# Block products of a hybrid decoder layer: accumulators copied into three fixed banks, a late fourth raw block, and five block pairs of eight in gate and up

## The chip, the core and the metric

One Trainium2 chip; the kernel runs on one core of it, as one program. The metric is device time in microseconds, the median of three runs. Of the engines, PE multiplies matrices, ACT, DVE and POOL work element by element, and SP issues transfers; ACT and POOL issue transfers too. Products accumulate in eight banks of PSUM, each 128 partitions by 512 fp32 numbers.

## The reference

One layer of a decoder in fp32, for 256 rows of width 2048: a half-step SwiGLU, a mixing part (four heads of differential attention and four of mLSTM behind one input projection, and one output projection), a second half-step SwiGLU, and a last norm.

```python
x = x + 0.5 * swiglu(rmsnorm(x, ffn1_norm[l]), ffn1_w_gate[l], ffn1_w_up[l], ffn1_w_down[l])
h = rmsnorm(x, mix_norm[l])
... = jnp.split(h @ w_in[l], split_idx, axis=-1)      # N_IN columns: q, k, v of both head groups, gates
...
x = x + jnp.concatenate([y_a, y_b], axis=-1) @ w_out[l]
x = x + 0.5 * swiglu(rmsnorm(x, ffn2_norm[l]), ffn2_w_gate[l], ffn2_w_up[l], ffn2_w_down[l])
return rmsnorm(x, final_norm)
# swiglu(h, g, u, d) = (silu(h @ g) * (h @ u)) @ d;  D_FF = 5632
```

Nearly all of the work is in the weights' products: gate and up are 2048 x 5632 each, down is 5632 x 2048, in both SwiGLUs.

## The kernel before

**Products.** An fp32 operand is cut into a high part `wh` (a cast by ACT, L122) and a low part `wl` (a subtraction by DVE, L123); for the rows `xs`, `xt` likewise. One product of 128 x 128 rows with a 128 x 512 weight tile is then three matmuls into one bank (L174, L175, L177: high by high, low by high, high by low). The weights come 128 rows of k at a time ("a k tile").

**Stages and blocks.** A stage is a `Paired`: two column chunks of 512, `wa` and `wb`, by both halves of the rows, so four accumulators, which the code calls n11 and n21 (`wa`, the two row halves) and n12 and n22 (`wb`). In the gate/up stages `wa` is a chunk of the gate weights and `wb` the same chunk of the up weights; in the down and mixing stages they are two neighbouring chunks. For `ns` pairs of k tiles the stage goes by a scheme of block products: sums of the four weight blocks (two k tiles by two chunks) and of the row blocks, and seven block products in place of eight. The other pairs (`rest`) are multiplied plainly in two passes, `second` for `wa` and `third` for `wb`. There are 45 such stages: 21 gate/up (one with `NP_FIRST` = 2 pairs, 20 with `NP` = 4; the very first chunk is plain), 16 down (3, 1, 3, 3 pairs, twice each in both SwiGLUs), 8 mixing.

`Chain.run` puts stages into one another: while the `third` pass of the stage ahead (its "stream") still runs, the leading block products of the next are put between its steps; then `end` takes the results of the stage ahead, `second` runs, and `half` takes n11 and n21.

**A block stage before.** `first` holds p1, p6, p7 and p5 in four banks of a pool of six. For each pair it loads four k tiles into `raw` (0, 1: `wa`; 2, 3: `wb`; L201), DVE makes two sums into `sums` (L426), a third into `raw[2]` (L430), and later POOL issues a DMA with accumulation, from SBUF to SBUF (L449):

```python
nc.gpsimd.dma_start(raw[:, 2, :], raw[:, 1, :], accum_op=ALU.add)
```

`p57` and `p16` multiply the sums. `combine` (L479 on ACT, L480 on DVE) and `combine_rest` (L486 to L490) join the four accumulators, partly in place; `second` adds the products of the unsummed blocks (`bare`, `upper`).

**Order.** The tile framework orders each engine's work by the order of the code and by priorities: `tc.high_priority(offset=AHEAD)` puts loads and splits 400 places ahead, `soon()` somewhat more. `ahead_of_splits` makes the fourth split behind a given place (`SLACK` = 4) wait in order until the given copy or joining operation has been issued on the same engine. The split weights have four buffers (`wsp`), raw blocks four (`wr`), raw plain pairs five (`wrp`); an engine takes its instructions strictly in order. The blocks of gate/up are loaded through POOL's queue (the first three chunks of each SwiGLU through SP's), the plain pairs through SP's.

Of the kernel before, what the change touches and what calls it, by code (L numbers as in the profile page):

```python
# [17 lines left out]
P = 128  # L18
# [15 lines left out]
NP = 4  # L34
# [14 lines left out]
SUMS = 4  # L49
ON_POOL = 3  # L50
FIRST_SUMS = 3
FLUSH = 3

# [5 lines left out]
def tile_trunk_layer(ctx: ExitStack, tc: tile.TileContext, x, xt, par, bias_if, lamv, fnorm,  # L59
# [10 lines left out]
    ps_acc = ctx.enter_context(tc.tile_pool(name="ps_acc", bufs=6, space=PSUM))  # L70
# [14 lines left out]
    touch = const.tile([1, 2], F32, name="touch")  # L85
# [3 lines left out]
    for _ in range(WARM):  # L89

        nc.tensor.matmul(warm, zeros[:, 0:P], zeros, start=True, stop=True)
# [58 lines left out]
    def load_w(src, pieces):  # L150

        raw = wr.tile([P, LK, src.shape[2]], F32, tag="raw", name=nm("raw"))
        with tc.high_priority(offset=AHEAD):
            o = 0
            for n in pieces:
                nc.sync.dma_start(raw[:, o:o + n, :], src[:, o:o + n, :])
                o += n
        return raw

# [43 lines left out]
    def load_unit(w, k):  # L203
        raw = wrp.tile([P, UK, w.shape[3]], F32, tag="rawp", name=nm("rawp"))
        with tc.high_priority(offset=AHEAD):
            load_pair(raw, w, k)
        return raw

    def units(accs, xp, w, nk, last_units=1, ahead=None, in_pieces=False, w0=0,
              fine=False):  # L210


        n = w.shape[3]
        accs += [ps_acc.tile([P, CW], F32, tag="acc", name=nm("acc"))[:, 0:n] for _ in range(NT)]

        def products(hbs, u, rh, rl):
            ks = [(t, u * UK + t) for t in range(UK)]
            mms([(accs[hb], *halves(xp, k, hb), rh[:, t, :], rl[:, t, :], k == 0, k == nk - 1, False)
                 for hb in hbs for t, k in ks])
# [3 lines left out]
        for u in range(nu):  # L223
# [5 lines left out]
            o = u * UK % LK  # L229
            if fine:  # L230
                rh, rl = split_w(load_unit(w, w0 * LK + u * UK), (UK,))
            else:
                if o == 0:
                    raw = load_w(w[w0 + u * UK // LK],
                                 (LK,) if not in_pieces else (UK, UK) if u else (1, 1, UK))
                rh, rl = split_w(raw[:, o:o + UK, :], (1, 1) if u == 0 and in_pieces else (UK,))
# [149 lines left out]
    def bank():  # L386
        return ps_acc.tile([P, CW], F32, tag="acc", name=nm("acc"))

    class Paired:

        def __init__(self, xp, wa, wb, nk, ns, w0=0, queue=nc.gpsimd):

            self.queue = queue
            self.xp, self.wa, self.wb, self.k0 = xp, wa, wb, w0 * LK
            self.ns, self.rest = ns, range(2 * ns, nk, UK)

            self.n = wa.shape[3]
            self.off = self.n - wb.shape[3]
            self.raws = []
# [5 lines left out]
        def first(self):  # L409


            n, off = self.n, self.off

            self.p1, self.p6, self.p7, self.p5 = (bank()[:, 0:n] for _ in range(4))
            last, sums = self.ns - 1, {}

            def load(j):
                raw = wr.tile([P, 4, n], F32, tag="raw", name=nm("raw"))
                self.raws.append(raw)
                with tc.high_priority(offset=AHEAD):  # L420
                    for i, w in enumerate((self.wa, self.wb)):
                        load_pair(raw[:, 2 * i:2 * i + 2, i * off:], w, self.k0 + 2 * j, self.queue)
                    if off:
                        nc.gpsimd.memset(raw[:, 2:4, 0:off], 0.0)
                    sums[j] = wrp.tile([P, 2, n], F32, tag="rawp", name=nm("sums"))
                    made = nc.vector.tensor_tensor(out=sums[j], in0=raw[:, 0:4:3, :],  # L426
                                                   in1=raw[:, 2:3, :].to_broadcast([P, 2, n]), op=ALU.add)
                    if len(splits) >= SUMS:
                        after(made, splits[-SUMS][1])
                    nc.vector.tensor_tensor(out=raw[:, 2, :], in0=sums[j][:, 0, :], in1=raw[:, 3, :], op=ALU.add)  # L430

            def halves_of(src):
                with tc.high_priority(offset=AHEAD):
                    t = pair_tiles(wsp, "w", [P, 2, n])
                    splits.append(split_weights(src, *t))
                return t

            def p57(j):
                f = halves_of(sums[j])
                jobs = [self.job(self.p7, j, S3, f, 1, j == 0, j == last), self.job(self.p5, j, S1, f, 0, j == 0, j == last)]  # L440
                for some in ([jobs[:1], jobs[1:]] if j == last else [jobs]):
                    mms(some)

            def p16(j):
                raw = self.raws[j]
                e = halves_of(raw[:, 0:3:2, :])
                mms([self.job(self.p1, j, A1, e, 0, j == 0, j == last), self.job(self.p6, j, S2, e, 1, j == 0, j == last)])
# [765 lines left out]
```

## Time and profile before

| | |
|---|---|
| runs | 1779.3, 1777.0, 1777.82 us, median 1777.82 |
| profiled execution, span | 1775.1 us (the page gives no other time of its own for it) |
| matmuls and transpositions on PE | 8012 |
| HBM read | 349.56 MB, 198 GB/s over the span |
| all transfers | 404.45 MB, mean 228 GB/s |

The page's slices, busy tenths of each fortieth of the span, show how even the work is:

```profile
PE   8999999999999999999999999999999999999998
DVE  7989897899889999997888999898897899889997
PEclk9999999999999999999999999999999999999999
DMA  9777977887797776666666566777987887887774
```

A row of the lines' view reads: line, engine, operation, output and inputs by their names in the program, shapes, count, busy time and the mean of one in ns, then the idle time ahead of them and what ended it. Line numbers in rows of before are those of the code above.

### The profile page before, as it was taken

The numbers are of one execution on the slowest core, as the hardware profiler recorded it, in microseconds if no ns is written. First come the engines' busy times: TensorE is split into PE (matmuls) and PEld (weight loads), VectorE is DVE, ScalarE is ACT, GpSimd is POOL, SyncE is SP. The second block draws the span as 40 slices with busy tenths as digits, with TensorE's granted clock in tenths as the row PEclk, the third lists the DMA queues.
The fourth block names the chain that finished last, engine by engine and source line by source line (L and its number), as shares of the span: only waits on it lengthen the run. The fifth ranks groups of instructions, "written<-read, shape, count | busy, mean of one in ns | idle before, by whom it ended". The sixth has DMA issues, their size and how long they took to land.

```text
span 1775.1 us, 23314 instructions
## 1 busy us (share of the span) xinstructions
PE 1759.9 (99%) x8012; PEld 1458.0 (82%) x8012; DVE 1588.4 (89%) x1933; ACT 1175.5 (66%) x1532; POOL 322.0 (18%) x489
## 2 busy tenths in 40 slices
PE   8999999999999999999999999999999999999998
PEld 6888888888888888987888788888888888888886
DVE  7989897899889999997888999898897899889997
ACT  7666665666666668776676776666665666666665
POOL 0011221211131211011112100012311211231110
PEclk9999999999999999999999999999999999999999
DMA  9777977887797776666666566777987887887774
GB/s 345 237 232 218 259 246 227 229 254 231 227 247 248 211 258 197 198 205 200 203 197 201 181 211 199 220 246 224 243 256 237 226 246 229 247 231 243 226 254 125
DMA packets 126614, 404.45 MB, mean 228 GB/s; under 512 B 14240, under 2 KB 15040, under 8 KB 126240
## 3 DMA queue, kind: packets, MB, share of 16 engines
q0 software_dynamic: 65584, 187.36, 40.8%
q1 hardware_dynamic: 59904, 213.53, 34.2%
q10 hardware_dynamic: 1008, 2.09, 0.3%
q8 instruction: 62, 1.02, 0.2%
q14 instruction: 56, 0.46, 0.1%
HBM read 349.56 MB, written 2.10 MB: 198 GB/s over the span
## 4 chain that ended last, share of the span: by engine, by line
PE 91%; DMA 3%; DVE 2%; issue 2%; POOL 1%; ACT 1%; SPq 0%; POOLq 0%; DVEq 0%; ACTq 0%
PE acc L174 29%; PE acc L177 29%; PE acc L175 29%; DMA raw<-in_wu_dram 3%; PE tr L337 1%; DVE wl L123 1%; DMA raw<-in_wg_dram 0%; DMA rawp<-in_wu_dram 0%; PE tr L278 0%; DVE sums L426 0%; PE sc L1005 0%; PE num L956 0%; POOL xres L321 0%; ACT wh L122 0%; PE tr L747 0%
## 5 line engine op out<-in xcount | busy, mean ns | idle before, releaser
L122 ACT CAST wh<-raw 128x1024 fp32r<-128x1024 f32 (+2 forms) x453 | 406.0, 907 | 250.0 <-PE acc L175 161.1
L174 PE MATMUL acc<-wh,xt 128*128 128x512 f32 (+2 forms) x1376 | 532.1, 388 | 0.2 <-ACT wh L122 0.2
L175 PE MATMUL acc<-wh,xt 128*128 128x512 f32 (+2 forms) x1376 | 530.9, 387 | 0.0
L123 DVE TENSOR_TENSOR wl<-raw,wh 128x1024 fp32r<-128x1024 f32 (+2 forms) x453 | 466.3, 1041 | 53.3 <-ACT wh L122 50.7
L123 DVE TENSOR_TENSOR wl<-rawp,wh 128x1024 fp32r<-128x1024 f32 (+3 forms) x360 | 430.9, 1201 | 54.3 <-ACT wh L122 44.9
L122 ACT CAST wh<-rawp 128x1024 fp32r<-128x1024 f32 (+3 forms) x360 | 372.4, 1036 | 150.0 <-PE acc L175 125.0
L174 PE MATMUL acc<-wh,xs 128*128 128x512 f32 (+2 forms) x1132 | 442.3, 392 | 4.3 <-ACT wh L122 3.4
L175 PE MATMUL acc<-wh,xs 128*128 128x512 f32 (+2 forms) x1132 | 436.8, 387 | 0.0
L177 PE MATMUL acc<-wl,xt 128*128 128x512 f32 (+2 forms) x1376 | 380.6, 387 | 0.0
L177 PE MATMUL acc<-wl,xs 128*128 128x512 f32 (+2 forms) x1132 | 352.1, 387 | 0.8 <-DVE wl L123 0.6
L174 PEld LDWEIGHTS acc<-wh,xt 128*128 128x128 f32 x1376 | 258.2, 188 | 52.8 <-ACT wh L122 0.7
L175 PEld LDWEIGHTS acc<-wh,xt 128*128 128x128 f32 x1376 | 258.3, 188 | 51.7
L177 PEld LDWEIGHTS acc<-wl,xt 128*128 128x128 f32 x1376 | 257.2, 188 | 52.1
L174 PEld LDWEIGHTS acc<-wh,xs 128*128 128x128 f32 x1132 | 212.4, 188 | 48.2 <-ACT wh L122 4.7
L177 PEld LDWEIGHTS acc<-wl,xs 128*128 128x128 f32 x1132 | 210.9, 188 | 46.0 <-DVE wl L123 3.4
L175 PEld LDWEIGHTS acc<-wh,xs 128*128 128x128 f32 x1132 | 212.7, 188 | 40.9
L449 POOL DMA_DIRECT2D raw<-raw x148 | 130.0, 879 | 637.9 <-DVE wl L123 603.8
L122 ACT CAST wh<-sums 128x1024 fp32r<-128x1024 f32 x148 | 155.4, 1050 | 98.5 <-PE acc L175 48.8
L426 DVE TENSOR_TENSOR sums<-raw 128x1024 f32<-128x1024 f32 x148 | 179.5, 1217 | 33.2 <-DMA raw<-in_wu_dram 32.9
L123 DVE TENSOR_TENSOR wl<-sums,wh 128x1024 fp32r<-128x1024 f32 x148 | 180.2, 1217 | 7.7 <-ACT wh L122 6.3
L430 DVE TENSOR_TENSOR raw<-sums,raw 128x512 f32<-128x512 f32 x148 | 101.4, 685 | 0.6
L201 POOL DMA_DIRECT2D raw<-in_wd_dram x80 | 42.6, 546 | 217.1 <-DVE wl L123 215.2
(206 smaller groups left out, 960.5 us busy)
## 6 DMA issues: line engine op xcount, KB each, us to landing
rawp<-in_wd_dram SPq DMA_DIRECT2D x96, 512.0 KB, 5.5
rawp<-in_wu_dram SPq DMA_DIRECT2D x94, 512.0 KB, 5.5
rawp<-in_wg_dram SPq DMA_DIRECT2D x86, 512.0 KB, 5.4
raw<-in_wd_dram POOLq DMA_DIRECT2D x80, 512.0 KB, 6.3
raw<-raw POOLq DMA_DIRECT2D x146, 256.0 KB, 5.2
raw<-in_wg_dram POOLq DMA_DIRECT2D x64, 512.0 KB, 6.3
raw<-in_wu_dram POOLq DMA_DIRECT2D x64, 512.0 KB, 7.5
rawp<-in_win_dram SPq DMA_DIRECT2D x44, 512.0 KB, 4.7
```

The source lines that it names most:

```text
L122: return (nc.scalar.copy(hi, src), nc.vector.tensor_tensor(out=lo, in0=src, in1=hi.bitcast(F32), op=ALU.subtract))
L123: nc.vector.tensor_tensor(out=lo, in0=src, in1=hi.bitcast(F32), op=ALU.subtract))
L174: nc.tensor.matmul(acc, lh, rh, start=first, stop=False, skip_group_check=on)
L175: nc.tensor.matmul(acc, ll, rh, start=False, stop=False, skip_group_check=on)
L177: nc.tensor.matmul(acc, lh, rl, start=False, stop=last, skip_group_check=on)
L201: queue.dma_start(dst, w[k // LK][:, k % LK:k % LK + 2, :])
L337: nc.tensor.transpose(tr[:, i, hb * P:(hb + 1) * P], hs[hb][:, k * P:(k + 1) * P], ident)
L426: made = nc.vector.tensor_tensor(out=sums[j], in0=raw[:, 0:4:3, :], in1=raw[:, 2:3, :].to_broadcast([P, 2, n]), op=ALU.add)
L430: nc.vector.tensor_tensor(out=raw[:, 2, :], in0=sums[j][:, 0, :], in1=raw[:, 3, :], op=ALU.add)
L449: nc.gpsimd.dma_start(raw[:, 2, :], raw[:, 1, :], accum_op=ALU.add)
```

## The change

- **Order of a block stage.** `leading` multiplies `wa`'s first block (A1) into a bank x and, after a sum by DVE over two blocks at once, S1 into a bank d, two pairs at a time, beside the stream of the stage ahead. Behind the stream, `sums` does S2 into x, on top of what stands there, a piece of the late block, S3 into x again, and the rest of the late block. `second` does the plain pairs of `wa` and, for each pair, B2 and S4 (`both`).
- **Accumulators.** ACT copies x three times, between two products that go into it: after A1 into the bank n11, after S2 into n12, after S3 into n21 (`copied`); the three banks are fixed, each of a tag of its own, and further products accumulate on what was copied there. d is copied to SBUF (`ds`), and DVE makes n12 = ds - n12 and x = ds - x (x is then n22). Six turning banks become three, besides the three fixed ones. Three matmuls of zeros start the fixed banks once.
- **Raw blocks.** A raw tile has three k tiles (`wa`'s first, both of `wb`) rather than four, and there are five of them, not four. `wa`'s second k tile of a pair is loaded late, through SP's queue, into a plain pair's buffer (`bare`, "late").
- **Sums.** The first two are one DVE operation in place. The third, raw[0] += raw[2], is a DMA with accumulation from SBUF to SBUF (by DVE in the down stages, `by_dma=False`). A fourth, raw[0] += `wa`'s second k tile, is a DMA with accumulation from HBM. The copy of before (`sums`, from the pool of plain pairs) is gone.
- **Five of eight.** `NP` becomes 5, so 20 gate/up stages have five pairs in blocks and three plain.
- **Besides.** The first chunk and wqk2 are loaded pair by pair (`load_unit`), and both halves of wqk2 share a bank.

Three places show how instructions move. First POOL's queue in the third gate/up chunk of the third part of the second half's SwiGLU weights `wg1` and `wu1` (raw_704 to raw_728 before, raw_761 to raw_776 after, are that chunk's raw blocks). Before, the last two blocks' loads and then its sums:

```order
L201 DMA raw_722_3561<-in_wg1_dram 128x1024
L201 DMA raw_722_3561<-in_wu1_dram 128x1024
L201 DMA raw_728_3588<-in_wg1_dram 128x1024
L201 DMA raw_728_3588<-in_wu1_dram 128x1024
L449 DMA raw_704_3471<-raw_704_3471 128x512
L449 DMA raw_713_3516<-raw_713_3516 128x512
L449 DMA raw_722_3561<-raw_722_3561 128x512
L449 DMA raw_728_3588<-raw_728_3588 128x512
```

After, the same place: the fifth block's loads, then five third sums and five fourth ones. (Line numbers of after are its own: L413 and L200 load, L455 is the third sum, L494 the fourth, L131 a cast, L464 a copy into a fixed bank, L173, L174 and L176 the three matmuls, L341 a transposition.)

```order
L413 DMA raw_776_3810<-in_wg1_dram 128x512
L200 DMA raw_776_3810<-in_wu1_dram 128x1024
L455 DMA raw_761_3724<-raw_761_3724 128x512
L455 DMA raw_762_3727<-raw_762_3727 128x512
L455 DMA raw_770_3776<-raw_770_3776 128x512
L455 DMA raw_771_3779<-raw_771_3779 128x512
L455 DMA raw_776_3810<-raw_776_3810 128x512
L494 DMA raw_761_3724<-in_wg1_dram 128x512
L494 DMA raw_762_3727<-in_wg1_dram 128x512
L494 DMA raw_770_3776<-in_wg1_dram 128x512
L494 DMA raw_771_3779<-in_wg1_dram 128x512
L494 DMA raw_776_3810<-in_wg1_dram 128x512
```

The loads stay ahead of the sums; the four sums became ten, and all third sums stand ahead of the first fourth one.

Second, ACT in the same chunk, where the accumulators are handed on. Before (acc_700 is p1, acc_702 is p7; wh are casts of block sums, of plain pairs `rawp` and of raw blocks):

```order
L122 CAST wh_736_3626<-sums_729_3591 128x1024
L122 CAST wh_740_3643<-rawp_739_3641 128x1024
L122 CAST wh_742_3661<-raw_704_3471 128x1024
L479 COPY u_732_3605<-acc_700_3467 128x512
L122 CAST wh_745_3673<-rawp_744_3671 128x1024
L122 CAST wh_754_3714<-raw_713_3516 128x1024
L487 COPY u3_738_3636<-acc_702_3469 128x512
```

After (acc_759 is x; the first casts of raw_761 to raw_776 are S2's, those behind the cast of the late block `late` S3's):

```order
L131 CAST wh_786_3853<-raw_761_3724 128x512
L131 CAST wh_786_3853<-raw_762_3727 128x512
L131 CAST wh_788_3867<-raw_770_3776 128x512
L131 CAST wh_788_3867<-raw_771_3779 128x512
L131 CAST wh_790_3881<-raw_776_3810 128x512
L131 CAST wh_793_3891<-late_795_3893 128x1024
L131 CAST wh_796_3903<-raw_761_3724 128x512
L131 CAST wh_796_3903<-raw_762_3727 128x512
L131 CAST wh_798_3915<-raw_770_3776 128x512
L131 CAST wh_798_3915<-raw_771_3779 128x512
L464 COPY accn12_792_3889<-acc_759_3722 128x512
L131 CAST wh_800_3927<-raw_776_3810 128x512
```

Before, the copy out of p1 stood with casts of 1024 columns around it; now S2's casts of 512 columns for five blocks, the late block's, and two of S3's stand ahead of the copy into n12.

Third, PE in the same chunk, where S3 begins. Before, behind the last step of the stream (acc_623 and acc_625), the last pair's products into p7 (acc_702) and p5 (acc_703):

```order
L177 MATMUL acc_625_3102<-wl_735_3611,xt_32_281 128x512 x2
L177 MATMUL acc_623_3100<-wl_735_3611,xt_32_281 128x512 x2
L174 MATMUL acc_702_3469<-wh_736_3626,xs_16_191 128x512
L175 MATMUL acc_702_3469<-wh_736_3626,xs_17_192 128x512
L177 MATMUL acc_702_3469<-wl_737_3627,xs_16_191 128x512
L174 MATMUL acc_703_3470<-wh_736_3626,xs_16_191 128x512
L175 MATMUL acc_703_3470<-wh_736_3626,xs_17_192 128x512
L177 MATMUL acc_703_3470<-wl_737_3627,xs_16_191 128x512
```

After, the last S2 products into x, those of the late block into n11, a transposition, and S3's first into x again:

```order
L173 MATMUL accn11_779_3820<-wh_793_3891,xs_7_138 128x512
L176 MATMUL acc_759_3722<-wl_789_3868,xs_20_198 128x512
L173 MATMUL acc_759_3722<-wh_790_3881,xs_29_242 128x512
L174 MATMUL acc_759_3722<-wh_790_3881,xs_30_243 128x512
L176 MATMUL acc_759_3722<-wl_791_3882,xs_29_242 128x512
L174 MATMUL accn11_779_3820<-wh_793_3891,xs_8_139 128x512
L173 MATMUL accn11_779_3820<-wh_793_3891,xs_9_145 128x512
L174 MATMUL accn11_779_3820<-wh_793_3891,xs_10_146 128x512
L341 MATMUL tr_814_3987<-ident_109,sg_754_3700 128x128
L173 MATMUL acc_759_3722<-wh_796_3903,xs_7_138 128x512
L176 MATMUL accn11_779_3820<-wl_794_3892,xs_7_138 128x512
L176 MATMUL accn11_779_3820<-wl_794_3892,xs_9_145 128x512
```

Between the last product of S2 (acc_759) and the first of S3 into the same bank now stand three products and a transposition in this chunk.

The diff, cut to its core (removed lines of `first`, `combine`, `combine_rest`, `bare` and `upper` are those shown in the code above):

```diff
-NP = 4
+NP = 5
+SEEDED = N11, N12, N21 = "n11", "n12", "n21"
...
-    slots = ctx.enter_context(tc.tile_pool(name="slots", bufs=21))
+    slots = ctx.enter_context(tc.tile_pool(name="slots", bufs=22))
...
-    wr = ctx.enter_context(tc.tile_pool(name="wr", bufs=4))
+    wr = ctx.enter_context(tc.tile_pool(name="wr", bufs=5))
...
-    ps_acc = ctx.enter_context(tc.tile_pool(name="ps_acc", bufs=6, space=PSUM))
+    ps_acc = ctx.enter_context(tc.tile_pool(name="ps_acc", bufs=3, space=PSUM))
...
+    def seeded(which):
+        return ps_acc.tile([P, CW], F32, tag=f"acc{which}", name=nm(f"acc{which}"), bufs=1)
+
+    for which in SEEDED:
+        nc.tensor.matmul(seeded(which), zeros[:, 0:P], zeros, start=True, stop=True)
...
+        one = banks is None
+        if one:
+            both = bank()
+            accs += [both[:, hb * n:(hb + 1) * n] for hb in range(NT)]
+        else:
+            accs += [b()[:, 0:n] for b in banks]
...
+        def load(self, j):
             n, off = self.n, self.off
+            raw = wr.tile([P, 3, n], F32, tag="raw", name=nm("raw"))
+            self.raws.append(raw)
+            k = self.k0 + 2 * j
+            with tc.high_priority(offset=AHEAD):
+                self.queue.dma_start(raw[:, 0, :], self.wa[k // LK][:, k % LK, :])
+                load_pair(raw[:, 1:3, off:], self.wb, k, self.queue)
...
+        def part(self, js, acc, xi, slot, first=False, last=False):
+            t = self.split_two([self.raws[j][:, slot, :] for j in js])
+            mms([self.job(acc, j, xi, t, i, first and j == 0, last and j == self.ns - 1, not first)
+                 for i, j in enumerate(js)])
+
+        def leading(self):
+            n = self.n
+            self.x, self.d = bank()[:, 0:n], bank()[:, 0:n]
+            for js in self.twos:
+                for j in js:
+                    self.load(j)
+                self.part(js, self.x, A1, 0, True, True)
+                if js[-1] == self.ns - 1:
+                    self.n11 = self.copied(N11)
                 with tc.high_priority(offset=AHEAD):
+                    for j in js:
+                        raw = self.raws[j]
+                        nc.vector.tensor_tensor(out=raw[:, 0:2, :], in0=raw[:, 0:3:2, :],
+                                                in1=raw[:, 1:2, :].to_broadcast([P, 2, n]), op=ALU.add)
+                self.part(js, self.d, S1, 0, True, True)
                 with tc.high_priority(offset=AHEAD):
+                    for j in js:
+                        raw = self.raws[j]
+                        if self.by_dma:
+                            nc.gpsimd.dma_start(raw[:, 0, :], raw[:, 2, :], accum_op=ALU.add)
+                        else:
+                            nc.vector.tensor_tensor(out=raw[:, 0, :], in0=raw[:, 0, :], in1=raw[:, 2, :], op=ALU.add)
+                yield
+
+        def copied(self, which):
+            t = seeded(which)[:, 0:self.n]
+            with soon():
+                ahead_of_splits(0, nc.scalar.copy(t, self.x))
+            return t
+
+        def bare(self, js):
...
+                raw = wrp.tile([P, UK, self.n], F32, tag="rawp", name=nm("late"))
...
+                    nc.sync.dma_start(raw[:, 0:len(js), :], self.wa[k // LK][:, ks, :])
...
+            mms([self.job(self.n11, j, A2, t, i, False, False, True) for i, j in enumerate(js)])
+
+        def sums(self):
+            with soon():
+                ds = wk("ds")[:, 0:self.n]
+                ahead_of_splits(0, nc.scalar.copy(ds, self.d))
+            for js in self.twos:
+                self.part(js, self.x, S2, 0)
                 with tc.high_priority(offset=AHEAD):
+                    for j in js:
+                        k = self.k0 + 2 * j + 1
+                        nc.gpsimd.dma_start(self.raws[j][:, 0, :], self.wa[k // LK][:, k % LK, :], accum_op=ALU.add)
+            self.n12 = self.copied(N12)
+            self.bare(self.twos[0])
+            for js in self.twos:
+                self.part(js, self.x, S3, 1)
+            self.n21 = self.copied(N21)
             with soon():
+                for t in (self.n12, self.x):
+                    ahead_of_splits(1, nc.vector.tensor_tensor(out=t, in0=ds, in1=t, op=ALU.subtract))
+            for js in self.twos[1:]:
+                self.bare(js)
...
+            def both(j):
+                t = self.split_two([self.raws[j][:, 0:3:2, :]])
+                mms([self.job(self.n21, j, B2, t, 0, False, False, True), self.job(self.n12, j, S4, t, 1, False, False, True)])
...
+            q = len(p.twos)
+            first = p.leading()
+            for i in range(q):
+                while done < min(self.steps - 1, -(-(i + 1) * self.steps // (q + 1))):
                     next(self.stream)
                     done += 1
+                next(first)
...
+            while done < self.steps:
+                next(self.stream)
+                done += 1
+            next(first, None)
             self.end()
+            p.sums()
             half(p.second())
...
-                p = Paired(hid, wd[c], wd[c + 1], n * 4, ns, done)
+                p = Paired(hid, wd[c], wd[c + 1], n * 4, ns, done, by_dma=False)
```

More of the change, by code (lines that the diff above doesn't have):

```diff
@@ L48 @@
 SLACK = 4
-SUMS = 4
 ON_POOL = 3
@@ L84, in tile_trunk_layer @@
     nc.vector.memset(zeros, 0.0)
-    touch = const.tile([1, 2], F32, name="touch")
+    touch = work.tile([1, 2], F32, tag="w", name="touch")
     nc.vector.memset(touch, 0.0)
@@ L384, in aside, with __init__ @@
             work.pop(0)()
-    def bank():
-        return ps_acc.tile([P, CW], F32, tag="acc", name=nm("acc"))
     class Paired:
-        def __init__(self, xp, wa, wb, nk, ns, w0=0, queue=nc.gpsimd):
-            self.queue = queue
+        def __init__(self, xp, wa, wb, nk, ns, w0=0, queue=nc.gpsimd, by_dma=True):
+            self.queue, self.by_dma = queue, by_dma
             self.xp, self.wa, self.wb, self.k0 = xp, wa, wb, w0 * LK
             self.ns, self.rest = ns, range(2 * ns, nk, UK)
+            self.twos = [range(j, min(j + 2, ns)) for j in range(0, ns, 2)]
             self.n = wa.shape[3]
@@ L407, in job @@
             return acc, xh[:, xi, :], xl[:, xi, :], w[0][:, wi, :], w[1][:, wi, :], first, last, on
-        def first(self):
+        def load(self, j):
             n, off = self.n, self.off
[L414 to L419, printed above, removed]
-                with tc.high_priority(offset=AHEAD):
[L421 to L432, printed above, removed]
-                with tc.high_priority(offset=AHEAD):
[L434 to L447, printed above, removed]
-                with tc.high_priority(offset=AHEAD):
-                    nc.gpsimd.dma_start(raw[:, 2, :], raw[:, 1, :], accum_op=ALU.add)
-            load(0)
-            p57(0)
-            yield
-            p16(0)
-            if last == 0:
-                self.combine()
-            for j in range(1, self.ns):
-                load(j)
-                if j < last:
-                    p57(j)
-                p16(j)
-                if j == last:
-                    self.combine()
-                if j % 2 and j < last - 1 or j == last:
-                    yield
-                if j == last:
-                    p57(j)
-            self.combine_rest()
-            yield
@@ new lines, in load, with split_two @@
+            self.raws.append(raw)
[3 more added lines that the diff above has]
+                load_pair(raw[:, 1:3, off:], self.wb, k, self.queue)
+                if off:
+                    nc.gpsimd.memset(raw[:, 1:3, 0:off], 0.0)
+        def split_two(self, srcs):
+            with tc.high_priority(offset=AHEAD):
+                t = pair_tiles(wsp, "w", [P, 2, self.n])
+                if len(srcs) == 1 and len(srcs[0].shape) == 3:
+                    made = split_weights(srcs[0], *t)
+                else:
+                    for i, src in enumerate(srcs):
+                        made = split_weights(src, t[0][:, i, :], t[1][:, i, :])
+                splits.append(made)
+            return t
```

111 lines of the change are left out of this document (39 added, 72 removed).

## The prediction

> **What bounds the kernel now.** I read the page's busy shares first, then what PE waits for, then PE's rows one by one, because a share of busy time says nothing about overlap.
>
> ```profile
> PE 1759.9 (99%) x8012; PEld 1458.0 (82%) x8012; DVE 1588.4 (89%) x1933; ACT 1175.5 (66%) x1532; POOL 322.0 (18%) x489
> ```
>
> The waits of PE over the whole span (engine, line, what it waited for: us, times, longest):
>
> ```profile
> PE acc L174 <- ACT wh L122: 3.6, 4, 1.2
> PE warm L91 <- DVE touch L86: 1.3, 1, 1.3
> PE acc L174 <- ACT xs L122: 1.0, 1, 1.0
> PE acc L177 <- DVE wl L123: 0.6, 2, 0.3
> ```
>
> They add up to 6.5 us: nothing but PE's own work is left to shorten. What one product costs is read from starts, in the timeline of PE:
>
> ```profile
> 500.48 0.39 PE L174 MATMUL acc<-wh,xs 128*128 128x512 f32 x1
> ...
> 504.79 0.62 PE L177 MATMUL acc<-wl,xs 128*128 128x512 f32 x2
> ...
> 505.92 0.39 PE L175 MATMUL acc<-wh,xs 128*128 128x512 f32 x1
> ```
>
> Each row lasts 0.39 us, but from the start at 500.48 to the start at 505.92 lie 24 products: 5.44 / 24 = 0.2267 us each. Last, two stretches: a gate/up chunk, and one with the down projections (length, then each engine's busy time; at the end clock, DMA share, GB/s).
>
> ```profile
> 398.00:439.80 41.80, 41.80 (x190) 34.67 (x189) 40.21 (x46) 27.39 (x33) 8.34 (x13) 1.00 0.74 219
> 470.00:520.00 50.00, 50.00 (x223) 41.39 (x222) 44.39 (x46) 33.51 (x39) 14.53 (x19) 1.00 0.92 248
> ```
>
> In both PE is never idle, at full granted clock. In the chunk DVE is at 40.2 of 41.8 us: the second bound, close behind. The DMA engines are far fuller in the down stretch (0.92) than in the chunk (0.74).
>
> **The change, part by part. Products.** NP goes from 4 to 5 for 20 chunks (nine of the first FFN, since its first is plain and its second keeps NP_FIRST, and eleven of the second). Each saves one block product of 3 matmuls: 60 x 0.2267 = 13.6 us, all on the path that sets the end. The row's 0.39 us would give 23.4; I don't take it, since rows overlap. The Trainium skill, "TensorE: Matmul & The Clock Gate", section "Wait — 56ns, not 53.3ns?", gives 215.7 ns from start to start for 512 columns on a warm array; the sum would be 12.9 us, and the trace's step is the longer one.
>
> **DVE and ACT.** Their prices, as groups by shape:
>
> ```profile
> L123 DVE TENSOR_TENSOR wl<-rawp,wh 128x1024 fp32r<-128x1024 f32 x340 | 414.1, 1221 | 51.7 <-ACT wh L122 42.4 <-PE acc L175 5.8
> L123 DVE TENSOR_TENSOR wl<-raw,wh 128x512 fp32r<-128x512 f32 x148 | 97.3, 686 | 4.1 <-ACT wh L122 3.6
> L426 DVE TENSOR_TENSOR sums<-raw 128x1024 f32<-128x1024 f32 x146 | 177.6, 1220 | 33.2 <-DMA raw<-in_wu_dram 32.9 <-issue 0.3
> L430 DVE TENSOR_TENSOR raw<-sums,raw 128x512 f32<-128x512 f32 x146 | 100.3, 687 | 0.6
> L480 DVE TENSOR_TENSOR u<-acc,u 128x512 f32<-128x512 f32 x44 | 30.2, 685 | 2.2 <-ACT u L479 1.3 <-PE acc L177 0.8
> L122 ACT CAST wh<-rawp 128x1024 fp32r<-128x1024 f32 x340 | 357.4, 1053 | 141.9 <-PE acc L175 120.6 <-issue 5.7 <-ACT wh L122 5.2
> L122 ACT CAST wh<-raw 128x512 fp32r<-128x512 f32 x148 | 87.8, 620 | 61.5 <-PE acc L175 60.6 <-DMA raw<-in_wg_dram 0.7
> L479 ACT COPY u<-acc 128x512 f32<-128x512 f32 x44 | 25.4, 578 | 4.0 <-PE acc L177 3.9
> ```
>
> DVE in one chunk, before: 4 blocks of 1.22 + 0.69 + 3 x 1.22 + 0.69 = 6.26, eight plain units of 1.22, four joining operations of 0.69: 37.6 us. After: 5 blocks of 1.22 (sum) + 4 x 0.69 (A1, S1, S2, S3 one by one) + 1.22 = 5.20, the late blocks 2 x 1.22 + 0.69, six plain units, two joining: 26.0 + 3.1 + 7.3 + 1.4 = 37.8. So +0.2 us for a chunk that PE does 0.68 us faster: DVE goes from 40.2 of 41.8 to 40.4 of 41.1. It stays below PE, so I cost it at nothing; the cover is 0.7 us a chunk, and without it PE would wait for wl. In the down projections (by_dma False) L430's operation stays and two joining ones go: lighter. ACT in one chunk: casts 4 x 3.78 + 8 x 1.05 and 2 copies, 24.7; after 5 x 3.53 + 2.73 + 6 x 1.05 and 4 copies, 29.0: 27.4 becomes some 31.7 of 41.1, hidden.
>
> **Loads and queues.** Apart from the sums, the weights' bytes stay. SP gets three late loads for a chunk, in the place of two plain ones, into the same five rawp buffers: prefetched, nothing. POOL:
>
> ```profile
> L449 POOL DMA_DIRECT2D raw<-raw x148 | 130.0, 879 | 637.9 <-DVE wl L123 603.8
> L201 POOL DMA_DIRECT2D raw<-in_wg_dram x64 | 38.8, 607 | 202.6 <-DVE wl L123 172.6 <-ACT wh L122 30.0
> ```
>
> A chunk had 8 loads and 4 sums, 8.4 us; now 10 and 10, 10 x 0.61 + 10 x 0.88 = 14.9 of 41 us. In POOL's order all loads of a chunk stand ahead of its first sum, and behind the waiting sums stand only loads whose buffers come free later: nothing is held up.
>
> **The third sum by DMA.** It puts a wait into the path: S2's cast must wait until raw[0] += raw[2] has landed, and that DMA starts only after DVE has split S1. The tight one is the fifth block, alone in its tile. PE has 12 stream products and 12 of S2 between its S1 and its S2: 5.44 us, and 0.68 for the S1 products. wsp's four pairs let the S1 split begin 15 products (3.4 us) before PE needs it; A1's split, the sum, cast and split (0.69, 1.22, 0.62, 0.69) take most of that, so it ends 0.6 to 1.4 us before PE starts. That makes 6.7 to 7.5 us; S2's cast and the splits behind it need 1.2 of them. The DMA has 5.5 to 6.3 us. ACT stands in order behind that cast: the late block and S3 wait with it. What the same kind of DMA took, issue to landing (median, last column), in the chunk and in the down stretch:
>
> ```profile
> raw<-raw POOLq DMA_DIRECT2D x5, 256.0 KB, 5.2
> ```
>
> ```profile
> raw<-raw POOLq DMA_DIRECT2D x7, 256.0 KB, 7.8
> ```
>
> By 5.2 it is hidden with 0.3 to 1.1 us to spare; by 7.8 it is 1.5 to 2.3 us late. I take the chunk's row, since it is the same stage, with 0.1 us a chunk for those that land late: 20 x 0.1 = 2.0 us, bounds 0 and 20 x 2.3 = 46. A gain is excluded: nothing waited for this sum before. The mixing projections have the same DMA with four and three blocks; their DMA share is lower, and I add nothing. The Trainium skill, "DMA: Bandwidth & Descriptors", section "Anatomy of one DMA — SWDGE (gpsimd) path", fits 2.0 us + bytes / 436e3 to a DMA, 2.6 us for 256 KB. By that nothing is ever late and the 2.0 us fall away; the trace's 5.2 does not agree.
>
> **DMA engines.** The queues on the page (packets, MB, share):
>
> ```profile
> q0 software_dynamic: 65584, 187.36, 40.8%
> q1 hardware_dynamic: 59904, 213.53, 34.2%
> ```
>
> q0 carries 136 MB of loads and 196 accumulating DMAs of 0.26 MB. With its loads at q1's 0.16% a MB, 21.8%, the rest is 19% for 196: 1.7 us of all engines each. A chunk has six more: 10 us of 41, so its share of 0.74 becomes 0.95 to 0.99. That is the down stretch's level, and the best reason against my choice. For it: around the fifth sum only sums and a plain load are under way, the chunk's own loads being long issued.
>
> **Accumulators handed on.** 45 block stages now copy x into n12 between S2 and S3, which write the same bank. In 37 PE has 6 products of the late block between, 1.36 us; the need is the end of the last product behind its step (0.39 - 0.23 = 0.16), a 512 cast that ACT is in (0.62) and the copy (0.58): 1.36. Nothing, but no spare. In the four chunks that end a part the order leaves 3 products and a transposition, 0.79 us: 0.6 late at most; in the four stages with one block a 1024 cast, 0.2 late. That is 3.1 at most, none if ACT stands ready, as its 120.6 us of waiting for PE in the cast's row suggest; I take 2.0. The copies into n11 and n21 have 1.6 us and more. Three seeding products run while the first weights load, where PE waits anyway; the one-bank unit of wqk2 has the same products: nothing.
>
> Sum: -13.6 + 2.0 + 2.0 = -9.6 on a span of 1775.1, so 1765.5; the median of the runs, 1777.8, stands 2.7 above that span, so 1768.2. Less than 3.6 us (0.2%) I call no change.
>
> **Rivals.** *Everything is hidden*: 1777.8 - 13.6 = 1764.2. For: PE lost 6.5 us in 1775 with DVE just as full; also where the skill's fit leads. Against: two waits without spare. *Handing-on eats the gain*: if ACT is in a 1024 cast at each copy, 0.43 longer, or DVE, in order, stands at the join of n12 until the copy ends and S3's splits come late, 45 stages lose 0.2 to 0.3 us: 9 to 13, so 1774 to 1777, no change. *The third sum comes late, slower*: full DMA engines take the fifth sum of each chunk from 5.2 to 7.8 us; 20 x 1.5 to 2.3 = 30 to 46 less 11.6 makes 1796 to 1812. It decides at 0.58 us a chunk, a landing of 6.1 to 6.9 us; at 0.8 us it is already past 1782. For: the share worked out above. Against: the lull at that place, and that a late PE also asks for less. *The change not doing what it says*: the built order has 60 512-wide products fewer, so no.
>
> **How the numbers follow.** My case (1766 to 1774) 0.43, all hidden 0.23, the hand-over's 0.15, the late sum 0.19. Faster by over 0.2% 0.66, within 0.15, slower 0.19. The likeliest case gives 1768. For 8 in 10 the range goes from 1763 (all hidden, and a first weight earlier) up to 1784: past no change, into the beginning of the late sum.
>
> **What would show it.** PE with 60 products fewer at the same 0.227 us step; DVE near 40 us and ACT near 31 in a chunk; in the waits of PE rows of ACT's casts and the copies of 4 us in all. Wrong if ACT's casts wait for the DMA raw<-raw for more than some 0.6 us a chunk and PE for them, if the DMA share of a chunk is near 1.0 with landings over 6.5 us, or if the first product after S2 starts late in most stages.

## The result, and the profile after

The change made the kernel slower: 1818.95 us (median of 4 runs) against 1778.34, ratio 1.0232 (95% interval 1.0215 to 1.0249). The forecast was 1768. The profiled execution spans 1816.4 us against 1775.1. The page's first line of after:

```profile
PE 1772.5 (98%) x7955; PEld 1443.7 (79%) x7955; DVE 1560.5 (86%) x2074; ACT 1261.0 (69%) x1939; POOL 471.1 (26%) x669
```

PE has 57 matmuls fewer (60 products less, three seeds more), and a share of 98% that looks as good as before. What PE waited for, over the whole span (engine, line, what it waited for: us, times, longest):

```profile
PE acc L173 <- ACT accn L464: 21.4, 27, 2.5
PE acc L173 <- ACT wh L131: 5.9, 4, 2.6
PE accn L173 <- ACT wh L131: 2.8, 3, 2.3
PE accn L173 <- ACT accn L464: 1.7, 4, 0.6
```

6.5 us of waits have become 34.3 (three rows of 2.5 us together are left out). The first row is new: products into x that wait for ACT's copy out of x (L464), 27 times. The view shows less than the loss, since a product's 0.39 us covers 0.16 us of each hold-up, and the product behind one starts some 0.11 us late as well. Counted from start to start, whatever steps of the 512-wide products exceed 0.2267 us adds up to 15.7 us before and 68.8 after. So 53.1 us were lost and 13.6 us of products saved; the 1.8 us that are missing to 41.3 lie in narrower products and transpositions.

Where they were lost: the same stretches of the program in both, cut at ACT's Silu of one chunk and the next (length, busy time of PE, PEld, DVE, ACT, POOL; clock, DMA share, GB/s). Before: the first block stage, a stretch with two down stages, a plain gate/up chunk, and the whole mixing part.

```profile
36.46:78.15 41.69, 41.69 (x189) 34.61 (x188) 39.84 (x53) 28.72 (x37) 1.77 (x2) 1.00 0.80 271
125.29:228.20 102.91, 102.91 (x459) 85.29 (x458) 90.11 (x94) 66.78 (x78) 26.31 (x38) 1.00 0.85 245
583.21:624.91 41.70, 41.70 (x189) 34.61 (x188) 40.12 (x47) 27.30 (x33) 7.73 (x12) 1.00 0.76 227
624.91:1109.78 484.87, 483.89 (x2321) 405.60 (x2320) 438.13 (x629) 337.85 (x522) 70.13 (x109) 1.00 0.66 204
```

After:

```profile
37.65:89.32 51.67, 44.74 (x189) 35.32 (x188) 37.05 (x54) 31.27 (x47) 3.52 (x4) 0.97 0.82 259
134.46:240.69 106.23, 103.83 (x456) 84.34 (x455) 90.62 (x108) 71.72 (x104) 32.90 (x47) 1.00 0.88 257
602.78:644.88 42.10, 41.83 (x186) 33.81 (x185) 39.87 (x53) 30.56 (x46) 12.89 (x19) 1.00 0.95 261
644.88:1141.35 496.47, 488.91 (x2320) 404.19 (x2319) 418.71 (x642) 355.22 (x607) 99.52 (x143) 1.00 0.75 217
```

A plain chunk is 0.4 us longer with three products fewer. The first block stage lost 10.0 us of the 53.1, the mixing part 11.3 with the same products as before, the seven stretches with down stages 18.7, the other chunks 11.9, and the start 1.2.

How one such wait comes about is seen in the first chunk of the fourth part of the first SwiGLU, behind the down stages of the third part. ACT's timeline of after (start, length, what; in brackets the idle time ahead and who ended it), from S2's casts to the copy into n12:

```profile
538.23 0.62 ACT L131 CAST wh<-raw 128x512 fp32r<-128x512 f32 x1 [0.41 <-DMA raw<-raw]
539.98 0.62 ACT L131 CAST wh<-raw 128x512 fp32r<-128x512 f32 x1 [1.12 <-DMA raw<-raw]
540.50 0.59 ACT L324 ACTIVATE part<-accn 128x512 f32<-128x512 f32 x1
540.99 1.04 ACT L131 CAST wh<-late 128x1024 fp32r<-128x1024 f32 x1
541.93 0.60 ACT L324 ACTIVATE part<-acc 128x512 f32<-128x512 f32 x1
542.42 0.59 ACT L488 COPY ds<-acc 128x512 f32<-128x512 f32 x1
542.88 2.19 ACT L131 CAST wh<-raw 128x512 fp32r<-128x512 f32 x4
544.97 0.60 ACT L464 COPY accn<-acc 128x512 f32<-128x512 f32 x1
```

PE in the same time: its last product of S2, the last ones of the late block, and the first of S3.

```profile
542.73 0.39 PE L176 MATMUL acc<-wl,xs 128*128 128x512 f32 x1
...
543.86 0.61 PE L176 MATMUL accn<-wl,xs 128*128 128x512 f32 x2
545.62 0.50 PE L173 MATMUL acc<-wh,xs 128*128 128x512 f32 x1 [1.14 <-ACT accn L464]
545.95 0.39 PE L174 MATMUL acc<-wh,xs 128*128 128x512 f32 x1
```

x was complete at 543.12, but ACT copied it only at 544.97, behind four casts of S3. And ACT was late there because the fifth block's S2 cast had waited until 539.98 for its third sum. S2 itself was not late for PE: that cast was done at 540.60, and PE came to it at 542.28. One wait delays ACT, the order of ACT's work hands the delay on, and another product pays.

### The profile page after: what moved, and what is told of

It is laid out like the page before. It is cut to its first block, busy times and chain, and to the rows that moved or that the text cites. A ratio compares the mean times of both kernels' runs of the same rounds, so it can differ in the third digit from the quotient of the medians.

```text
span 1816.4 us, 24465 instructions
## 1 busy us (share of the span) xinstructions
PE 1772.5 (98%) x7955; PEld 1443.7 (79%) x7955; DVE 1560.5 (86%) x2074; ACT 1261.0 (69%) x1939; POOL 471.1 (26%) x669
## 3 DMA queue, kind: packets, MB, share of 16 engines
q8 instruction: 62, 1.02, 0.2%
## 5 line engine op out<-in xcount | busy, mean ns | idle before, releaser
L131 ACT CAST wh<-raw 128x512 fp32r<-128x512 f32 (+1 forms) x845 | 568.9, 705 | 307.2 <-DVE raw L448 144.2
L132 DVE TENSOR_TENSOR wl<-raw,wh 128x512 fp32r<-128x512 f32 (+1 forms) x845 | 646.9, 793 | 112.8 <-ACT wh L131 97.6
L131 ACT CAST wh<-rawp 128x1024 fp32r<-128x1024 f32 (+3 forms) x324 | 334.0, 1033 | 112.3 <-PE accn L174 59.0
L173 PE MATMUL accn<-wh,xt 128*128 128x512 f32 (+2 forms) x888 | 350.5, 397 | 2.1 <-ACT accn L464 1.3
L174 PE MATMUL accn<-wh,xt 128*128 128x512 f32 (+2 forms) x888 | 343.7, 389 | 0.0
L173 PE MATMUL acc<-wh,xs 128*128 128x512 f32 (+2 forms) x712 | 280.0, 394 | 28.3 <-ACT accn L464 21.4
L174 PE MATMUL acc<-wh,xs 128*128 128x512 f32 (+2 forms) x712 | 275.6, 388 | 0.0
L176 PE MATMUL accn<-wl,xt 128*128 128x512 f32 (+2 forms) x888 | 258.0, 389 | 0.2
L176 PE MATMUL acc<-wl,xs 128*128 128x512 f32 (+2 forms) x712 | 233.0, 388 | 0.0
L455 POOL DMA_DIRECT2D raw<-raw x128 | 110.8, 873 | 465.6 <-DVE wl L132 379.2
L173 PE MATMUL accn<-wh,xs 128*128 128x512 f32 (+1 forms) x576 | 225.8, 393 | 2.7 <-ACT wh L131 2.3
L174 PE MATMUL accn<-wh,xs 128*128 128x512 f32 (+1 forms) x576 | 223.9, 390 | 0.0
L448 DVE TENSOR_TENSOR raw<-raw 128x1024 f32<-128x1024 f32 x168 | 199.7, 1216 | 0.4
L173 PEld LDWEIGHTS accn<-wh,xt 128*128 128x128 f32 x888 | 166.1, 188 | 42.0 <-ACT accn L464 5.6
L176 PEld LDWEIGHTS accn<-wl,xt 128*128 128x128 f32 x888 | 165.9, 188 | 37.2 <-DVE wl L132 3.5
L174 PEld LDWEIGHTS accn<-wh,xt 128*128 128x128 f32 x888 | 166.8, 188 | 31.8
L173 PEld LDWEIGHTS acc<-wh,xs 128*128 128x128 f32 x712 | 133.8, 188 | 70.3 <-ACT accn L464 34.9
L176 PE MATMUL accn<-wl,xs 128*128 128x512 f32 (+1 forms) x576 | 182.6, 390 | 0.7 <-DVE wl L132 0.5
L176 PEld LDWEIGHTS acc<-wl,xs 128*128 128x128 f32 x712 | 133.1, 188 | 31.4 <-DVE wl L132 3.8
L174 PEld LDWEIGHTS acc<-wh,xs 128*128 128x128 f32 x712 | 133.9, 188 | 25.9 <-DVE xs L132 0.4
L173 PEld LDWEIGHTS accn<-wh,xs 128*128 128x128 f32 x576 | 108.7, 189 | 26.6 <-ACT wh L131 3.2
```

Source lines behind the costliest of these rows:

```text
L131: return (nc.scalar.copy(hi, src), nc.vector.tensor_tensor(out=lo, in0=src, in1=hi.bitcast(F32), op=ALU.subtract))
L132: nc.vector.tensor_tensor(out=lo, in0=src, in1=hi.bitcast(F32), op=ALU.subtract))
L173: nc.tensor.matmul(acc, lh, rh, start=first, stop=False, skip_group_check=on)
L174: nc.tensor.matmul(acc, ll, rh, start=False, stop=False, skip_group_check=on)
L176: nc.tensor.matmul(acc, lh, rl, start=False, stop=last, skip_group_check=on)
L448: nc.vector.tensor_tensor(out=raw[:, 0:2, :], in0=raw[:, 0:3:2, :], in1=raw[:, 1:2, :].to_broadcast([P, 2, n]), op=ALU.add)
```

## The experiments

Two theories. *Place*: ACT takes the copies too late, behind casts that nobody needs yet. *Late sum*: the accumulating DMA of the third sum comes late and ACT with it. A third, that the DMA engines are full, stood beside them. The kernel before was run again beside each new kernel; its medians lay between 1776.88 and 1778.35 us, so differences between medians below are good to some 1.5 us. The ratios are to that kernel.

**The copy into n12 earlier.** Only an order: the copy gets a slack of its own, 2 in place of `SLACK` = 4. In the traces three of S3's casts then stand ahead of it in a chunk, where five stood, or four in the chunks that begin or end a part.

```diff
-            self.n12 = self.copied(N12)
+            self.n12 = self.copied(N12, 2)
...
```

> Only the order changes: the copy into n12 has to stand ahead of the second split behind it, not the fourth. Theory of the place (ACT takes the copy behind casts of S3 and of later blocks, and S3 waits for it): the 21.4 us that PE's products into x wait for that copy, and some 0.2 us of slower products behind each of 27 waits, go for the most part, so 1792 to 1800 us. Rival, late third sum (ACT is late because S2's casts wait for the accumulating DMA, 28.2 us in 32 waits): the copy is late wherever it stands, 1812 to 1819. Rival, DMA engines full: nothing changes, 1815 to 1822.

Measured: 1800.67 us, ratio to before 1.0139 (1.0122 to 1.0156), 18 us better. PE's waits for that copy:

```profile
PE acc L173 <- ACT accn L464: 6.4, 11, 1.0
```

21.4 us have become 6.4. The time is 0.7 us above the place theory's range, but an order alone gave a third of the 53.1 us back, which neither rival allows.

**The last group's third sum by DVE.**

```diff
-                        if self.by_dma:
+                        if self.by_dma and js[-1] < self.ns - 1:
```

> The third sum of the last group of blocks (the fifth block alone in gate and up, one or two blocks in the mixing projections) is done by DVE, no longer by a DMA, in the old order of copies. Theory of the place: ACT's waits for that DMA go (28 us of ACT's time), but the copy still stands behind S3's casts; in the stages where S2's last cast waited 1.1 us the stall shrinks, 1805 to 1815. Rival, late third sum: most of the 53 us goes, below 1790. A third way: DVE has 0.69 us more in a chunk and becomes the bound, above 1819.

Measured: 1796.26 us, 1.0108 (1.0093 to 1.0123), 23 us better: more than the place theory gave it, less than the late sum's. The row of the copy, whose order is unchanged:

```profile
PE acc L173 <- ACT accn L464: 7.5, 5, 3.6
```

Most of the same wait goes when ACT is no longer held by the DMA. The two edits don't cure the same places best: in the example above the early copy leaves 1.02 of the 1.14 us, since ACT is late all the same, and the sum by DVE leaves nothing; in the first block stage the early copy takes the whole wait for the copy away, and with the sum by DVE alone it grows from 2.45 to 3.6 us. The mixing part falls from 496.47 to 488.52 us, so the sum cost 8 us there.

**Both.**

> Both edits. Place theory: the copy's order carries most, so within 8 us of the kernel with the early copy alone, 1786 to 1796. Late third sum: most comes with the second edit, 1770 to 1785, and the first adds little to it. If the two waits stand behind one another, the gains add up or more.

Measured: 1788.26 us, 1.0063 (1.0048 to 1.0078). The single gains, 18 and 23, would add up to 41; together they are 31. So some 10 us stood behind both in a row: either cure takes them. The time lies in the place theory's range (1786 to 1796), but 12 us below the early copy alone, where that theory allowed 8; and the gains add up to less than their sum, not to more. So none of the three expectations was met fully.

**Four pairs again**, `NP = 4` in the changed kernel.

> The changed kernel with four pairs in blocks in gate and up, as before the change, so 60 products more (13.6 us). If the loss belongs to the scheme (place of the copy, every stage), the stalls stay and it takes 1825 to 1835. If it belongs to the fifth block (its third sum alone in its group, five pairs of sums for the DMA engines, five casts of S3 ahead of the copy), the stalls of 20 stages go, 1780 to 1800.

Measured: 1859.13 us, 1.0463 (1.0441 to 1.0485): 40 us slower than with five, where 13.6 us of products were to be expected, and outside both expected ranges. The loss is not the fifth block's. With four pairs the last group has two blocks; my reading, which no run tests by itself, is that both third sums then begin later and are needed sooner. ACT's waits for them, 28.2 us in 32 times with five pairs, became:

```profile
ACT wh L131 <- DMA raw<-raw: 82.6, 60, 5.3
```

**The copy into n21 early too**, on top of both.

```diff
-            self.n21 = self.copied(N21)
+            self.n21 = self.copied(N21, 2)
```

> The kernel with both edits, and the copy into n21 too has to stand ahead of the second split behind it. In the first block stage PE waited 3.0 us for that copy, which stood behind a cast of a block whose fourth sum was still under way, and then made ten products at half pace (1.7 us). Place theory: those 4.7 us go, 1782 to 1785. Rival (the fourth sum from HBM is late by itself, B2 and S4 wait for it wherever the copy stands): no change, 1786 to 1790.

Measured: 1785.16 us, 1.0036 (1.0023 to 1.005), at the upper edge of the place theory's range and 0.8 us short of the rival's; the medians' 3 us lie within the runs' spread. For the place theory speaks the first block stage, which fell from 48.61 to 45.83 us.

**All third sums of the mixing part by DVE**, on top of that (`by_dma=False` there).

> As the one before, and all third sums of the eight mixing stages by DVE. The stretch of the mixing part was still 3.7 us over the kernel before. If the DMA's latency holds the rest: 2 to 4 us less, 1778 to 1782. Rival, DVE in order: up to 16 more operations of 0.69 us ahead of splits, equal or up to 4 us slower than the one before.

Measured: 1788.53 us, 1.0062 (1.0046 to 1.0079): no gain, 3.4 us above the one before, as the rival had it. The DMA sums of the mixing part's groups that aren't last cost nothing that these runs show.

**Four pairs in this mended kernel.**

> The one before with four pairs in blocks in gate and up. If the waits for the third sum and for the copies were what made four pairs 40 us slower than five in the kernel as changed, only the 60 products remain: 10 to 18 us more than five pairs. Rival (with four pairs the first product of S2 comes too early behind S1 for any order of copies): 25 us more or beyond.

Measured: 1798.0 us, 1.011 (1.0095 to 1.0125), 9.5 us above five pairs by the medians, just under the expected 10 to 18. The spans of the profiled executions differ by 13.9 (1796.9 against 1783.0), but these were the slowest of one kernel's four runs and the fastest of the other's. Counted from start to start in them, both kernels lose about the same (33.3 and 34.8 us), so the 40 us are gone and the products remain. Not place by place, though. The same chunk as above, here with four pairs, takes exactly the time of before:

```profile
590.88:632.59 41.71, 41.71 (x189) 34.61 (x188) 37.28 (x47) 28.52 (x40) 9.62 (x14) 1.00 0.84 240
```

With five pairs and both copies early it takes no less, for three products fewer:

```profile
587.15:628.92 41.77, 41.77 (x186) 33.73 (x185) 40.24 (x54) 30.40 (x45) 12.45 (x18) 1.00 0.92 261
```

Four pairs lose instead in the stretches with down stages: the one shown above takes 106.90 us, against 102.94 with five pairs and both copies early, and 0.7 of these 4 us are products.

**No third sum by DMA at all**, with both copies early.

```diff
-                        if self.by_dma and js[-1] < self.ns - 1:
+                        if False:
```

> As the one with both copies early, and every third sum by DVE, in gate and up too: four more operations of 0.69 us in a chunk, so DVE goes from 40.0 to 42.7 of 41.3 us. If DVE is the second bound with no spare, 20 chunks of 1.4 to 2.7 us: 1810 to 1838. Rival, the DMA's latency costs more than DVE's time: equal or faster than with the DMA for the first groups, 1775 to 1785.

Measured: 1839.46 us, 1.0332 (1.0304 to 1.036). The chunk:

```profile
601.69:645.77 44.08, 42.10 (x186) 33.60 (x185) 42.97 (x56) 30.29 (x45) 10.25 (x16) 1.00 0.74 216
```

The time is just above the range for a full DVE. Four operations of 0.69 us made the chunk 2.3 us longer, and DVE is busy for 42.97 of its 44.08 us: it has become the bound. The DMA share fell from 0.92 to 0.74, and emptier DMA engines helped nothing here.

**The fifth block's double sum parted**, on the kernel with both copies early. There a chunk still lost 0.34 to 0.74 us against 41.03 (41.71 less three products). DVE's timeline of that kernel at the fifth block: A1's splits, the double sum of 1.22 us, and the split of S1.

```profile
413.73 1.28 DVE L132 TENSOR_TENSOR wl<-raw,wh 128x512 fp32r<-128x512 f32 x2
414.93 1.22 DVE L448 TENSOR_TENSOR raw<-raw 128x1024 f32<-128x1024 f32 x1
416.89 0.69 DVE L132 TENSOR_TENSOR wl<-raw,wh 128x512 fp32r<-128x512 f32 x1 [0.74 <-ACT wh L131]
```

```diff
+                        if len(js) == 1:
+                            nc.vector.tensor_tensor(out=raw[:, 0, :], in0=raw[:, 0, :], in1=raw[:, 1, :], op=ALU.add)
...
+                        if len(js) == 1:
+                            nc.vector.tensor_tensor(out=raw[:, 1, :], in0=raw[:, 2, :], in1=raw[:, 1, :], op=ALU.add)
```

> As the kernel with all three edits (early copies into n12 and n21, last group's third sum by DVE), and where the last group is one block the double sum of 1.22 us is parted into two of 0.69 us, of which the one for S3 stands behind the third sum. In the chunks, PE still lost 0.34 to 0.74 us against the 41.03 us that its products take, at S1 of the fifth block, which waits in a row for A1's split, the double sum, a cast and a split. If that chain is the rest of the chunks' loss, 20 chunks get 0.3 to 0.5 us back: 1775 to 1779. Rival: DVE is full (40.0 of 41.3 us, 0.16 us more here), no gain, 1785 to 1788.

Measured: 1780.87 us, 1.002 (1.001 to 1.003), 4.3 us better, less than expected. The edit holds wherever the last group is one block, so in down and mixing stages of one and three pairs too. In the chunk the split of S1 now follows without a gap of its own; ahead of it stand both single sums, the second one (L462) too, which the code has behind the third sum:

```profile
413.57 0.68 DVE L449 TENSOR_TENSOR raw<-raw 128x512 f32<-128x512 f32 x1
414.29 0.69 DVE L462 TENSOR_TENSOR raw<-raw 128x512 f32<-128x512 f32 x1
415.00 0.69 DVE L132 TENSOR_TENSOR wl<-raw,wh 128x512 fp32r<-128x512 f32 x1
```

**The copy of d later**, behind the copy into n12.

> As the kernel with all three edits, and ACT's copy of d to SBUF stands behind the copy into n12 instead of ahead of S2's casts. If ACT's queue is what makes the copies late where evacuations of the stage ahead stand in it too, the 3.6 us of PE's remaining waits for the copy into n12 go, with 0.25 us behind each of six: 1780 to 1783. Rival: d's bank is needed, and the products of the next plain pairs or the join wait for it: 1786 or more.

Measured: 1786.33 us, 1.0054 (1.0037 to 1.0071): no gain, as the rival had it, without its cause being shown.

**All of these, and the fourth sum of two-pair stages by DVE.**

> Both of these, and in the first block stage and the one of wqk (two pairs) DVE does the fourth sum from the late block's tile, not a DMA from HBM. The first block stage is 4 us over the kernel before; if the late landing of its sums at a time of full DMA engines makes that, 2 to 4 us go. With the other two: 1770 to 1776, below the kernel before. Rival: the sums of the single gains do not add since DVE is full, 1778 to 1783.

Measured: 1778.95 us, 1.0009 (1.0 to 1.0019): neither faster nor slower than the kernel before, in the rival's range; that DVE is full, the rival's reason, is not shown by it. The first block stage came to 43.31 us (45.83 without), the mixing part to 487.48. The gains did not reach the expected sum: 27.6 us of hold-ups over 0.06 us each are left where the kernel before has 13.3, spread over many places, and that is what the 13.6 us of products had brought.

**The copy ahead of all of S3's splits** in stages of one to three pairs, with the copy of d back at its place.

> As the kernel with early copies, the last group's third sum by DVE, the parted double sum, and DVE's fourth sum in the stages of two pairs, with the copy of d at its old place; and in stages of one to three pairs (the down projections, most of the mixing stages) the copy into n12 has to stand ahead of the very first split of S3. The kernel with the other edits still has 2.9 us of waits for that copy in 5 of those stages and its slower products behind them. If the copy's place holds them: 1774 to 1778. Rival (the casts of S3 behind the copy then come late for PE, 0.62 us and more in 20 stages): 1782 to 1790.

Measured: 1785.69 us, 1.0041 (1.0027 to 1.0055): in the rival's range. Casts are late now, and the rows of PE's waits for the copy are gone:

```profile
PE accn L173 <- ACT wh L131: 7.7, 7, 1.9
PE acc L173 <- ACT wh L131: 5.3, 6, 1.3
```

The reason given for that range holds in four stages, not in 20. Of the 10.2 us between the profiled spans of this kernel and that of the previous run (6.7 by the medians), 7.8 lie in the two stretches with the down stages of one pair (90.25 and 87.79 us, against 85.49 and 84.73). There the one cast of S3 stands behind the copy, and PE waits for it and for the casts that follow. The other stretches with down stages differ by less than 0.8 us either way. So the number was met, and its reason only in part: in the stages of one pair the copy has no room to move further ahead.

## Why the prediction was wrong, point by point

- **Products, -13.6 us: right.** 60 fewer, and four against five pairs in the mended kernel differ by 9.5 us in the runs and 13.9 in the spans, though in single chunks some of it was lost again at S1 of the fifth block.
- **DVE, ACT, POOL, DMA engines in a chunk: right, or near.** Forecast 40.4, 31.7 and 14.9 us and a share of 0.95 to 0.99; measured 39.87, 30.56 and 12.89, and 0.95. That DVE has no more room than that was shown by the kernel without DMA sums.
- **"Accumulators handed on", 2.0 us: this step failed.** The waits for copies alone measured 23.1 us (21.4 and 1.7), and their order was worth 18. The need was worked out from the copy's own chain (one cast and the copy) on the ground that ACT "stands ready", as its waiting for PE over the span suggested. That sum is an average over the span. At this place the copy into n12 began 0.1 to 3.2 us after x was complete, over 1.3 us in 17 of the 45 stages, and the order of instructions decided what that meant. The rows of ACT's order ahead of the prediction show it: four of S3's casts stand there between the late block's and the copy (the text beside them says two), where the sum had room for one.
- **"The third sum by DMA", 2.0 us: this step failed too**, by 23 us over all stages together with what hung on it, though its landing in the chunks was not slower but faster than forecast. Landings in a late chunk's stretch, in the changed kernel (KB, median us from issue to landing):

```profile
raw<-raw POOLq DMA_DIRECT2D x6, 256.0 KB, 3.6
```

  The forecast compared the landing (5.2 us) with PE's need of S2. It said that ACT's later work waits behind that cast, and put no price on it. The price was there: ACT waited 28.2 us for these sums, and PE paid at S3. At S2 itself PE waited for such a cast in two stages alone, 2.60 us in the first block stage and 1.64 us in one chunk. The slack was mis-added as well: 15 products (3.4 us) less the four operations (3.22 us) leave 0.2 us, not 0.6 to 1.4, so by its own rows the DMA had 5.1 us for a landing of 5.2. That did no harm, since the fifth sums of the 20 chunks landed after 3.3 to 6.1 us, 3.5 by the median.
- **"The mixing projections ... I add nothing": failed.** 11.3 us lost there, 8 of them by the last group's DMA sum. The reason given, a lower DMA share, speaks of the landing; what counts, as I read it, is how few products stand between S1 and S2 of the last group. No run tests that by itself.
- **The first block stage was not priced at all**, and lost 10.0 us. With two pairs there is one group, so its third sums have little time, and they run while loads fill the DMA engines (a share of 1.00 from 60 to 63.5 us). The second of them landed 6.9 us after its issue, and here S2 itself was late, by the 2.60 us named above. ACT's timeline of after shows the chain: the cast of S2 that waits for the third sum, and the copy into n12 behind a cast for B2 and S4, later products, which waits for the fourth sum.

```profile
61.07 1.14 ACT L131 CAST wh<-raw 128x512 fp32r<-128x512 f32 x2 [3.27 <-DMA raw<-raw]
62.12 1.05 ACT L131 CAST wh<-rawp 128x1024 fp32r<-128x1024 f32 x1
65.19 1.04 ACT L131 CAST wh<-raw 128x1024 fp32r<-128x1024 f32 x1 [2.02 <-DMA raw<-in_wg_dram]
66.14 0.58 ACT L464 COPY accn<-acc 128x512 f32<-128x512 f32 x1
```

- **The rivals.** The late sum was put at 1796 to 1812 us with landings of 6.1 to 6.9 as its condition; the time went past it, and the condition was reached in one of the 20 chunks alone (6.1 us, the chunk with the 1.64 us). The hand-over was put at 9 to 13 us, some half of what it was. They were weighed as two cases, and the runs show them as one chain through ACT.
- **The Trainium skill.** "DMA: Bandwidth & Descriptors", section "Anatomy of one DMA — SWDGE (gpsimd) path", has the fit from which the forecast worked out 2.6 us, an estimate, for such a DMA; the 3.6 us of this chunk are nearer to it than the 5.2 us that were used. That it would then be hidden did not follow.

The early copy into n12 and the last group's sum by DVE show the cause of some 31 of the 53.1 us. What stays open: where the last 14 us of the best version go in detail, and why the later copy of d brought nothing.

## What to carry to other kernels

An engine's idle share over the span says nothing about where it stands at one instruction: read the instructions that stand between the one that is needed and the one that waits on that engine, in its order, and add them up. If one of them waits for a transfer, all behind it do, and the product that pays may belong to another operand. Two short chains without spare that run through the same engine are one chain: they must be priced together, and in the stages with the fewest blocks first.

## What of the hardware was not expected

After a stop of 2.45 us in the first block stage, in a time when PE had little to do, its clock halved: the granted clock over these 3.6 us is 0.56, and the products start 0.43 us apart. A longer stop just before, of 2.60 us up to 61.74, had left it at 1.00. Before the halving and after it:

```profile
60.00:63.50 3.50, 1.76 (x8) 1.36 (x9) 1.78 (x3) 2.10 (x3) 0.79 (x1) 1.00 1.00 301
64.00:66.60 2.60, 0.33 (x2) 0.00 (x0) 1.41 (x2) 1.41 (x2) 0.00 (x0) 1.00 1.04 390
66.60:70.20 3.60, 3.42 (x9) 2.69 (x10) 1.82 (x2) 1.09 (x3) 0.00 (x0) 0.56 0.83 244
```

```profile
66.78 0.58 PE L173 MATMUL acc<-wh,xs 128*128 128x512 f32 x1 [2.45 <-ACT accn L464]
67.15 0.63 PE L174 MATMUL acc<-wh,xs 128*128 128x512 f32 x1
67.58 0.63 PE L173 MATMUL acc<-wh,xs 128*128 128x512 f32 x1
68.01 0.63 PE L174 MATMUL acc<-wh,xs 128*128 128x512 f32 x1
...
70.14 0.55 PE L173 MATMUL accn<-wh,xs 128*128 128x512 f32 x1
```

From 66.78 to 70.14 eight steps take 3.36 us where 0.2267 us each make 1.81, so the wait of 2.45 us cost some 1.5 us more. The Trainium skill, "TensorE: Matmul & The Clock Gate", section "What's actually happening", has the halved clock after an idle window of about 3.4 us; here a shorter stop, in a stretch that was mostly idle, was enough.

The traces show what it went by. The halving lasts 3.41 us (67.04 to 70.46), and all changes of the clock within a run lie a whole number of such stretches apart. With the 14 traces cut on that grid, up to the end of the work, PE was busy for 0.13 to 1.79 us in the 18 stretches just ahead of a halving, and for 1.60 us or more in every other one at full clock. Here the stretch with most of the 2.60 us stop had 1.88 us of work, the next one, with the 2.45 us, 0.96. In the last experiment a stop of 1.87 us was enough, in a stretch with 1.54 us of work. So the clock went by the busy share of the stretch, the border lying near half of it, and not by the length of one stop.
